# Hybrid attention encoder on one core: branch B's blocks and heads reordered and spaced, head normalisation on ScalarE, first two output blocks interleaved in K

## The chip, the core and the metric

One core of a Trainium2 chip runs the whole kernel. It has TensorE (PE: matmuls; PEld: its weight loads), VectorE (DVE), ScalarE (ACT), GpSimd (POOL) and SyncE (SP), which here issues every DMA. Each engine works through its own instructions strictly in the order in which the program gave them, and waits at an instruction until the semaphores that it needs have come. The metric is the device time of one execution in microseconds, the median over several runs.

## The reference, cut to what matters

256 tokens, width 2048, two layers, everything in float32. Each layer is

```python
h = rmsnorm(x, pre_norm_g[l])
proj = h @ w_in[l]                      # 2048 x 17920: q, k, v of three mixers, gates
ya = neighbourhood_attention(qa, ka, va, rpb[l])          # branch A, 8 heads
yb = gqa_attention(axial_rope(rmsnorm(qb)), axial_rope(rmsnorm(kb)), vb)   # branch B, 8 query heads, 2 key heads
yc = dilated_mixture(qc, kc, vc)                          # branch C, 4 output heads out of 12
merged = ga * ((ya * silu(za)) @ wa) + gb * ((yb * silu(zb)) @ wb) + gc * ((yc * silu(zc)) @ wc)
x = x + rmsnorm(merged @ w_out[l], post_norm_g[l])
```

where ga, gb, gc are sigmoids of the last 3 x 2048 columns of the projection. A head of branch A or B is a 256 x 256 score matrix, a softmax and a product with v.

## The kernel before, in words

**Blocks and chunks.** All large products go through one list, `stream` (L714 to L719). A block (`Blk`) makes 512 output columns for the 256 tokens, in two PSUM tiles `acc` of 128 tokens (T = 0 and 1); its K dimension is cut into chunks of 256 rows (`kc`). A chunk is one weight tile `raw` of 128x1024, which arrives by DMA and is split into a high part `wh` (ScalarE, L195) and a low part `wl` (VectorE, L200). Each chunk is twelve matmuls: two halves of K, two halves T, and three products high*high, low*high and high*low (`mm3`, L170 to L172). Numbered from 0, a layer has 352 chunks: ten blocks of branch C (chunks 0 to 79), eight of A (80 to 143), five of B (144 to 183), four merges of 34 chunks each (184 to 319: three gate blocks and the projections of branches A, C, B), and four output blocks (320 to 351).

**Order around the chunks.** The emission order is written out by hand. Before chunk i, `ahead(i)` (L203) emits the DMAs of `raw` up to chunk i+6, the `wh` of chunk i+3 and the `wl` of chunk i+2. After chunk i comes one `slot()` (L100): it takes up to two steps of the evacuations in `evq`, one step of each running job in `active`, and then starts one job: from `light` if one is due, otherwise from `heavy` if nothing is in `light` and the counter `cool` has come down to 0. The number that stands with a heavy job is the cool that follows it, the spacing of heads in chunks.

**A head** (`head_job`, L389; `job_c` for branch C) is a job whose steps lie one slot apart. Step 0: scores `sc` on TensorE, the row maximum `nm` on VectorE, two exponentials `sp` on ScalarE with their sums. Step 1: `norm` (L374), which makes `rsum` and multiplies the probabilities with it, on VectorE. Step 3: `turn` (L143), the transposition: VectorE transposes 32x32 squares into `tt`, a DMA writes `tt` to DRAM (`turn`), and at step 5 a DMA reads it back as `tx`. Step 7: `tx` is split into `pp` high and low. Step 9: the product `o` on TensorE, then `z` on VectorE; the fourth head of a unit also splits the gated result into `yTh` (ScalarE) and `yTl` (VectorE).

**`tr_job`** (L304) transposes a projected block in the same way (q, k, the gates, the merged tokens) and then, for branch B's queries, calls `then`, which puts the four heads of that block into `heavy`. `evac_qb` (L536) evacuates branch B's queries: four sums of squares on ScalarE (`junk`, L531), the mean `hss`, the rotary products `tok`, `s`, `tok` on VectorE (`rope`, L509) and the factor `bf`.

**Output blocks** (L628) read the merged tokens `mT`, one tile for each merge: chunk kc of any output block reads merge kc // 2. The last merge is transposed while the first output block runs.

Of the kernel before, what the change touches and what calls it, by code (L numbers as in the profile page):

```python
# [10 lines left out]
F32 = mybir.dt.float32  # L11
# [3 lines left out]
AF = mybir.ActivationFunctionType  # L15
ALU = mybir.AluOpType
# [4 lines left out]
P = 128  # L21
# [10 lines left out]
class Blk:  # L32


    def __init__(self, w, nk, stat, evac, pre=None):
        self.w, self.nk, self.stat, self.evac, self.pre = w, nk, stat, evac, pre
        self.nc = nk // 2
        self.lag = False
        self.far = False
        self.before = {}  # L40
        self.after = {}

# [5 lines left out]
def trunk(ctx, tc, x, xT, wpack, wbr_a, wbr_b, wbr_c, wout, pre_g, qk_g, bgate, post_g, abias,  # L48
          ident_d, rope_d, dist_d, x1, out):
    nc = tc.nc  # L50
# [4 lines left out]
    mm = ctx.enter_context(tc.tile_pool(name="mm", bufs=4, space=PSUM))  # L55
# [34 lines left out]
    evq, light, heavy, active = deque(), deque(), deque(), []  # L90
# [84 lines left out]
    stream = []  # L175
# [55 lines left out]
    def layer(l):  # L231
# [66 lines left out]
        def proj(nb, evac, pre=None):  # L298
            b = Blk([wpack[l, nb, kc] for kc in range(8)], 16, stat_h, evac, pre)
            blocks.append(b)  # L300
            return b


        def tr_job(dst, tok, n=4, then=None):  # L304


            tx = []
            yield from turn([tok[:, T] for T in range(2)], n, tx)
            for T in range(2):
                src = turned(tx[0], T, n)  # L310
                v = lambda t: squares(t[:, 0:n], T)
                if isinstance(dst, tuple):
                    split(src, v(dst[0]), v(dst[1]))
                else:
                    nc.scalar.copy(v(dst), src)
            if then:
                then()

        def evac_qk(store, key, which, two):
# [54 lines left out]
        def norm(p, sm, n, rsh):  # L374

            r = small.tile([P, n], F32, name="rsum")
            nc.vector.reciprocal(r, sm)
            nc.vector.tensor_tensor(out=r, in0=r, in1=rsh, op=ALU.mult)
            for i in range(n):
                nc.vector.tensor_scalar(p[:, i], p[:, i], r[:, i:i + 1], None, op0=ALU.mult)  # L380

        def gate(zb, hh, o, last):
            y = SZ[zb][:, hh]
# [40 lines left out]
        def job_a(u, hh, bias):  # L424
            q, k, v = QT["a", u], KT["a", u], V["a", u]
            d = slice(hh * P, (hh + 1) * P)
            return head_job(("a", u), hh, cols(q, ALL, hh), cols(k, ALL, hh),
                            lambda kk: cols(v, ALL, kk, d), bias=bias)

        def job_b(u, hh):  # L430
            d = slice(u * P, (u + 1) * P)
            return head_job(("b", u), hh, cols(QT["b", u], ALL, hh), cols(KT["b"], ALL, u),
                            lambda kk: cols(V["b"], ALL, kk, d), f=S["bf", u][:, hh])

        def job_c(hh, dist):

            q, k = [QT["c", g] for g in range(3)], [KT["c", g] for g in range(3)]
            v = [V["c", g] for g in range(3)]
            d = slice(hh * P, (hh + 1) * P)
            ps_ = []  # L440
            for T in range(2):
                c = slice(T * P, (T + 1) * P)
                sc = aux.tile([P, 1, 512], F32, name="sc")
                mm3(sc[:, 0, 0:256], cols(q[0], ALL, hh, c), cols(k[0], ALL, hh), True, True)
                for g in (1, 2):
                    nc.tensor.matmul(sc[:, 0, 128 + g * 128:256 + g * 128], lhsT=q[g][:, hh, c],  # L446
                                     rhs=k[g][:, hh, c], start=True, stop=True)
                sp = U("sp", [2, 1, 512])
                s, p = sp[:, 0], sp[:, 1]
                nc.vector.scalar_tensor_tensor(s[:, 0], dist[:, T], -(2.0 ** (-8.0 * (hh + 1) / 12)),  # L450
                                               sc[:, 0], op0=ALU.mult, op1=ALU.add)
                sm = softmax(s, p, 1, 512)
                ps_.append(p)
                yield
                norm(p, sm, 1, S["rsh"][T])
                if T == 0:
                    yield
            yield
            pp = U("pp", [2, 2, 256], FR)
            ph, pl = pp[:, 0], pp[:, 1]  # L460
            px = U("px", [2, 256])
            tx = []
            yield from turn([ps_[T][:, 0] for T in range(2)], 4, tx)
            for T in range(2):
                src = turned(tx[0], T, 4)
                split(src[:, 0:2], squares(ph, T), squares(pl, T))
                nc.scalar.copy(squares(px, T), src[:, 2:4])
            yield
            yield
            o = aux.tile([P, 256], F32, name="o")  # L470
            for kk in range(2):
                mm3(o, cols(v[0], ALL, kk, d), (ph[:, kk], pl[:, kk]), kk == 0, False)
            for T in range(2):
                c = slice(T * P, (T + 1) * P)
                for g in (1, 2):
                    nc.tensor.matmul(o[:, c], lhsT=v[g][:, T, d], rhs=px[:, g - 1, c],
                                     start=False, stop=T == 1 and g == 2)
            gate(("c", 0), hh, o, hh == 3)


        def a_unit(u):
            bias = {}

            def pre():
                for i in range(2):
                    b = U("abias", [2, 2, 256])
                    nc.sync.dma_start(out=b, in_=abias[l, u, i].rearrange("p (h t k) -> p h t k", h=2, t=2))
                    bias[i] = b

            def go():  # L490
                for hh in range(4):
                    heavy.append((2, job_a(u, hh, bias[hh // 2][:, hh % 2])))
            proj(18 + u, evac_z(("a", u)))
            proj(0 + u, evac_qk(QT, ("a", u), "rss", True))
            proj(2 + u, evac_qk(KT, ("a", u), "rs", True))
            proj(4 + u, evac_v(("a", u), True, go), pre=pre)
# [39 lines left out]
        def evac_qb(u):  # L536
            tok = {}

            def f(T, ps):
                if T == 0:  # L540
                    tok[0] = U("tok", [2, 512])
                    S["bf", u] = small.tile([P, 4, 2], F32, name="bf", bufs=2)
                    QT["b", u] = pair("qk", [4, 256])
                y = head_norm(ps, T, 4)
                yield from rope(tok[0][:, T], ps, T, 4, 0)
                nc.vector.tensor_scalar(S["bf", u][:, :, T], y, S["rss"][T], None, op0=ALU.mult)
                if T == 1:
                    later(tr_job(QT["b", u], tok[0],
                                 then=lambda: heavy.extend((2, job_b(u, hh)) for hh in range(4))), 1)
            return f  # L550

        def evac_kvb(T, ps):
# [17 lines left out]
        def go_c():  # L570
            dist = U("dist", [2, 512])
            nc.sync.dma_start(out=dist, in_=dist_d)
            for hh in range(4):
                heavy.append((4, job_c(hh, dist)))


        def merge(nb):
# [93 lines left out]
            proj(15 + g, evac_v(("c", g), g == 0, go_c if g == 2 else None))  # L671
        a_unit(0)
        a_unit(1)
        proj(20, evac_z(("b", 0)))
        b0 = proj(21, evac_z(("b", 1)))
        b0.at("after", (0, 1), b_tables)
        proj(8, evac_kvb)
        proj(6, evac_qb(0))
        proj(7, evac_qb(1))
        for nb in range(4):  # L680
            merge(nb)
        for nb in range(4):
            lastb = out_block(nb)
        lastb.lag = True

        if l == 0:
# [27 lines left out]
    for l in range(DEPTH):  # L714
        bl, S = layer(l)
        S0 = S0 or S
        for b in bl:
            for kc in range(b.nc):
                stream.append((b, kc))  # L719


    nc.sync.dma_start(out=gpre, in_=pre_g)
    for i in range(8):
        nb, k = divmod(i, 2)
# [23 lines left out]
    while i < len(stream):  # L748
        b = stream[i][0]
        n = b.nc  # L750
        if b.lag:
            a = [(i + k, 0) for k in range(n)]
            c = [(i + k, 1) for k in range(n)]
            order += a[:LAG]
            for k in range(n - LAG):
                order += [a[LAG + k], c[k]]
            order += c[n - LAG:]
        else:
            order += [(i + k, T) for k in range(n) for T in range(2)]
        i += n  # L760

    ps = {}
    for i, T in order:
        b, kc = stream[i]
        for f in b.before.get((kc, T), ()):
            f()
        if i > 0:
            ahead(i)
        if kc == 0:
            ps[T] = mm.tile([P, 512], F32, name="acc")  # L770
        run_half(i, T, ps[T])
        for f in b.after.get((kc, T), ()):
            f()
        if kc == b.nc - 1:
            evq.append(b.evac(T, ps[T]))
        if T == 1 or b.lag:
            slot()
    while evq or active or light:
# [99 lines left out]
```

## Time and profile before

| | before |
|---|---|
| median of 3 runs | 2043.8 us (2043.03 to 2046.01) |
| the profiled execution, whole | 2045.3 us |
| its span, first to last instruction | 2043.2 us |
| PE busy | 2014.1 us (99%) |
| VectorE busy | 1294.6 us (63%) |
| ScalarE busy | 959.0 us (47%) |
| mean granted TensorE clock | 0.994 |

The span is what the trace covers; 2.1 us lie around it. PE busy counts the time in which at least one matmul is under way, whatever clock it was granted, so that a slower stretch counts as busy too. The other engines' idle time matters only where TensorE waits for them.

### The profile page before, as it was taken

The page shows a single profiled execution, that of the slowest core. Times are in us where ns is not written, and L with a number is a line of the kernel's source. Part 1 is how long each engine was busy: PE and PEld are TensorE (multiplying, and loading weights), DVE is VectorE, ACT ScalarE, POOL GpSimd, SP SyncE. Part 2 cuts the span into 40 slices and gives each one's busy share as a digit, 9 for nine tenths or more (in the row PEclk, how much of TensorE's full clock was granted, in tenths as well). Part 3 has the DMA queues.
Part 4 walks back from the last instruction along what each step waited for, and adds up shares of the span by engine and source line. Part 5 has one row for each costly group of instructions (what it writes and reads, how often), then busy time and mean ns, then how long its engine had stood idle before and what let it go on. Part 6 is the DMA issues. An engine that isn't in the chain of part 4 may idle for free.

```text
span 2043.2 us, 24560 instructions
## 1 busy us (share of the span) xinstructions
PE 2014.1 (99%) x9098; PEld 1666.8 (82%) x9098; DVE 1294.6 (63%) x1645; ACT 959.0 (47%) x1402; POOL 24.0 (1%) x31
## 2 busy tenths in 40 slices
PE   9999999999999999999999999999999999999998
PEld 7888888888778888887888888888887788888876
DVE  6654587776786564645565555786767865646554
ACT  7544445445453444342564453555454544443422
POOL 0000000000000000000000000000000000000000
PEclk9999999999999999999999999999999999999999
DMA  8776375866666756667557664768665666656572
GB/s 326 258 263 258 137 287 203 290 215 257 217 215 225 263 199 218 226 212 272 185 167 275 240 249 144 277 226 303 211 259 191 240 217 245 217 195 225 201 283 72
DMA packets 171719, 468.05 MB, mean 229 GB/s; under 512 B 15440, under 2 KB 58576, under 8 KB 171600
## 3 DMA queue, kind: packets, MB, share of 16 engines
q1 hardware_dynamic: 171600, 466.50, 63.4%
q8 instruction: 71, 1.16, 0.2%
q14 instruction: 48, 0.39, 0.1%
HBM read 427.11 MB, written 39.32 MB: 228 GB/s over the span
## 4 chain that ended last, share of the span: by engine, by line
PE 89%; DVE 5%; ACT 2%; DMA 2%; issue 1%; SPq 0%; DVEq 0%; ACTq 0%; POOLq 0%
PE acc L171 29%; PE acc L172 29%; PE acc L170 29%; DMA tx<-turn 2%; DVE wl L200 1%; DVE tt L148 1%; ACT wh L195 1%; DVE nm L364 0%; ACT sp L369 0%; DVE pp L132 0%; PE sc L172 0%; PE sc L446 0%; DVE sp L380 0%; PE o L172 0%; PE o L171 0%
## 5 line engine op out<-in xcount | busy, mean ns | idle before, releaser
L200 DVE TENSOR_TENSOR wl<-raw,wh 128x1024 fp32r<-128x1024 f32 (+1 forms) x706 | 830.7, 1213 | 145.4 <-ACT wh L195 144.9
L171 PE MATMUL acc<-wl,hTh 128*128 128x512 f32 x2240 | 876.3, 391 | 7.4 <-DVE wl L200 7.4
L170 PE MATMUL acc<-wh,hTh 128*128 128x512 f32 x2240 | 877.4, 392 | 0.4 <-ACT wh L195 0.4
L172 PE MATMUL acc<-wh,hTl 128*128 128x512 f32 x2240 | 874.2, 390 | 0.0
L195 ACT CAST wh<-raw 128x1024 fp32r<-128x1024 f32 (+1 forms) x706 | 703.4, 1043 | 346.9 <-DMA raw<-in_wpack_dram 217.8
L171 PEld LDWEIGHTS acc<-wl,hTh 128*128 128x128 f32 x2240 | 422.2, 188 | 97.9 <-DVE wl L200 12.7
L172 PEld LDWEIGHTS acc<-wh,hTl 128*128 128x128 f32 x2240 | 422.1, 188 | 88.1
L170 PEld LDWEIGHTS acc<-wh,hTh 128*128 128x128 f32 x2240 | 422.3, 189 | 86.1 <-ACT wh L195 0.9
L170 PE MATMUL acc<-wh,yTh 128*128 128x512 f32 x320 | 124.5, 389 | 0.0
L171 PE MATMUL acc<-wl,yTh 128*128 128x512 f32 x320 | 124.5, 389 | 0.0
L172 PE MATMUL acc<-wh,yTl 128*128 128x512 f32 x320 | 124.5, 389 | 0.0
L594 ACT ACTIVATE g<-g 128x512 f32<-128x512 f32 x48 | 30.4, 634 | 192.8 <-DVE g L593 192.8
L593 DVE SCALAR_TENSOR_TENSOR g<-acc,rsx,bg 128x512 f32<-128x512 f32 x48 | 35.9, 747 | 128.7 <-PE acc L172 128.5
L170 PE MATMUL acc<-wh,mTh 128*128 128x512 f32 x256 | 101.6, 397 | 3.8 <-ACT mTh L130 3.8
L172 PE MATMUL acc<-wh,mTl 128*128 128x512 f32 x256 | 101.0, 395 | 0.0
L171 PE MATMUL acc<-wl,mTh 128*128 128x512 f32 x256 | 101.0, 394 | 0.0
L369 ACT ACTIVATE sp<-sp,nm 128x256 f32<-128x256 f32 (+1 forms) x48 | 27.6, 576 | 116.4 <-DVE nm L364 116.4
L605 DVE SCALAR_TENSOR_TENSOR g<-g,acc 128x512 f32<-128x512 f32 x48 | 32.8, 684 | 68.1 <-PE acc L172 68.1
L148 DVE STREAM_TRANSPOSE tt<-tok 128x512 f32<-128x512 f32 (+1 forms) x72 | 73.5, 1060 | 0.0
L171 PEld LDWEIGHTS acc<-wl,yTh 128*128 128x128 f32 x320 | 60.1, 188 | 12.4
L172 PEld LDWEIGHTS acc<-wh,yTl 128*128 128x128 f32 x320 | 60.1, 188 | 12.4
L170 PEld LDWEIGHTS acc<-wh,yTh 128*128 128x128 f32 x320 | 60.1, 188 | 12.3
(111 smaller groups left out, 1078.0 us busy)
## 6 DMA issues: line engine op xcount, KB each, us to landing
raw<-in_wpack_dram SPq DMA_DIRECT2D x558, 512.0 KB, 6.5
raw<-in_wo_dram SPq DMA_DIRECT2D x64, 512.0 KB, 9.2
turn<-tt SPq DMA_DIRECT2D x50, 512.0 KB, 3.0
tx<-turn SPq DMA_DIRECT2D x50, 512.0 KB, 5.5
raw<-in_wa_dram SPq DMA_DIRECT2D x32, 512.0 KB, 3.4
raw<-in_wb_dram SPq DMA_DIRECT2D x32, 512.0 KB, 4.6
turn<-tt SPq DMA_DIRECT2D x34, 256.0 KB, 2.2
tx<-turn SPq DMA_DIRECT2D x34, 256.0 KB, 4.3
```

Of the source, the lines that this page charges most:

```text
L148: nc.vector.transpose(out=tt[:, :, T].rearrange("p j (h a) -> p h j a", h=n), in_=srcs[T].rearrange("p (h b j) -> p h j b", h=n, j=4))
L170: nc.tensor.matmul(out_, lhsT=lh, rhs=rh, start=first, stop=False)
L171: nc.tensor.matmul(out_, lhsT=lh, rhs=rl, start=False, stop=False)
L172: nc.tensor.matmul(out_, lhsT=ll, rhs=rh, start=False, stop=last)
L195: nc.scalar.copy(HI[i][:, k], RAW[i][:, k])
L200: nc.vector.tensor_tensor(out=LO[i][:, k], in0=RAW[i][:, k], in1=f32(HI[i][:, k]), op=ALU.subtract)
L369: nc.scalar.activation(p[:, i], sc[:, i], AF.Exp, bias=nm[:, i:i + 1], scale=1.0 if f is None else f[:, i:i + 1], accum_out=sm[:, i:i + 1])
L593: nc.vector.scalar_tensor_tensor(g, ps, S["rs"][T], BG[i], op0=ALU.mult, op1=ALU.add)
L594: nc.scalar.activation(g, g, AF.Tanh, scale=0.5)
L605: nc.vector.scalar_tensor_tensor(G[i][:, T], G[i][:, T], 1.0, ps, op0=ALU.add, op1=ALU.mult)
```

## The change

1. `norm` multiplies the probabilities on ScalarE (an activation with function Copy and `rsum` as its scale) where it did on VectorE. `rsum` itself stays on VectorE.
2. The spacing of heads goes from 2 to 3 chunks in branches A and B, and from 4 to 5 in branch C.
3. `tr_job` waits two more slots between its split and `then`, so that branch B's first head comes two slots behind the split of its queries.
4. Branch B's blocks go from z0, z1, kv, q0, q1 to z0, kv, q0, z1, q1.
5. The first two output blocks are interleaved in K: six chunks of block 0, six of block 1, the last two of block 0, the last two of block 1.

```diff
             if then:
+                yield
+                yield
                 then()
...
             for i in range(n):
-                nc.vector.tensor_scalar(p[:, i], p[:, i], r[:, i:i + 1], None, op0=ALU.mult)
+                nc.scalar.activation(p[:, i], p[:, i], AF.Copy, scale=r[:, i:i + 1])
...
-                    heavy.append((2, job_a(u, hh, bias[hh // 2][:, hh % 2])))
+                    heavy.append((3, job_a(u, hh, bias[hh // 2][:, hh % 2])))
...
-                                 then=lambda: heavy.extend((2, job_b(u, hh)) for hh in range(4))), 1)
+                                 then=lambda: heavy.extend((3, job_b(u, hh)) for hh in range(4))), 1)
...
-                heavy.append((4, job_c(hh, dist)))
+                heavy.append((5, job_c(hh, dist)))
...
-        proj(20, evac_z(("b", 0)))
-        b0 = proj(21, evac_z(("b", 1)))
+        b0 = proj(20, evac_z(("b", 0)))
         b0.at("after", (0, 1), b_tables)
         proj(8, evac_kvb)
         proj(6, evac_qb(0))
+        proj(21, evac_z(("b", 1)))
         proj(7, evac_qb(1))
...
-        for nb in range(4):
-            lastb = out_block(nb)
+        outs = [out_block(nb) for nb in range(4)]
+
+        outs[0].mate, outs[1].mated = outs[1], True
+        lastb = outs[3]
...
         for b in bl:
-            for kc in range(b.nc):
-                stream.append((b, kc))
+            if b.mate:
+                m = b.mate
+                stream += [(b, kc) for kc in range(6)] + [(m, kc) for kc in range(6)]
+                stream += [(c, kc) for c in (b, m) for kc in range(6, 8)]
+            elif not b.mated:
+                stream += [(b, kc) for kc in range(b.nc)]
...
-            ps[T] = mm.tile([P, 512], F32, name="acc")
+            ps[b, T] = mm.tile([P, 512], F32, name="acc")
```

Branch B's second query block ends with chunk 183 in both. ScalarE's queue from the evacuation of its first half (the first four `junk`) is, before:

```order
L531 ACTIVATE junk,hss<-acc 128x128 x4
L130 ACTIVATE qkh<-tx 128x4x128 x2
L369 ACTIVATE sp,sm<-sc,nm,bf 128x256 x2
L195 CAST wh<-raw 128x1024
L531 ACTIVATE junk,hss<-acc 128x128 x4
L195 CAST wh<-raw 128x1024 x4
```

and in the changed kernel, from the exponentials of branch B's second head on:

```order
L373 ACTIVATE sp,sm<-sc,nm,bf 128x256 x2
L197 CAST wh<-raw 128x1024
L535 ACTIVATE junk,hss<-acc 128x128 x4
L384 ACTIVATE sp<-sp,rsum 128x256 x2
L197 CAST wh<-raw 128x1024
L535 ACTIVATE junk,hss<-acc 128x128 x4
```

The split of the first queries (`qkh`) and the first exponentials have left this place for an earlier one; the normalisation of the second head (L384) stands between the two groups of squares. VectorE's queue at the same place, in the changed kernel:

```order
L368 TENSOR_REDUCE nm<-sc 128x2
L370 TENSOR_TENSOR nm<-nm,bf 128x2
L202 TENSOR_TENSOR wl<-raw,wh 128x1024
L537 TENSOR_SCALAR hss<-hss,rsx 128x4
L517 TENSOR_TENSOR tok<-acc,ropeg 128x512
L525 TENSOR_TENSOR s<-acc,ropeg 128x8x32 x2
L527 TENSOR_TENSOR tok<-tok,s 128x512
L381 RECIPROCAL rsum<-sm 128x2
L382 TENSOR_TENSOR rsum<-rsum,rsx 128x2
L202 TENSOR_TENSOR wl<-raw,wh 128x1024
L550 TENSOR_SCALAR bf<-rs_y,rsx 128x4
L537 TENSOR_SCALAR hss<-hss,rsx 128x4
```

The second head's `rsum`, for which ScalarE's L384 waits, stands behind the rotary products of the first half. VectorE's queue where branch B's first unit ends (`yTl`), before:

```order
L384 TENSOR_TENSOR z<-o,z 128x256
L132 TENSOR_TENSOR yTl<-z,yTh 128x1024
L132 TENSOR_TENSOR pp<-tx,pp 128x2x128 x2
L148 STREAM_TRANSPOSE tt<-sp 128x2x4x32 x2
L377 RECIPROCAL rsum<-sm 128x2
L378 TENSOR_TENSOR rsum<-rsum,rsx 128x2
L380 TENSOR_SCALAR sp<-sp,rsum 128x256 x2
L200 TENSOR_TENSOR wl<-raw,wh 128x1024
```

and in the changed kernel:

```order
L388 TENSOR_TENSOR z<-o,z 128x256
L134 TENSOR_TENSOR yTl<-z,yTh 128x1024
L150 STREAM_TRANSPOSE tt<-sp 128x2x4x32 x2
L368 TENSOR_REDUCE nm<-sc 128x2
L370 TENSOR_TENSOR nm<-nm,bf 128x2
L202 TENSOR_TENSOR wl<-raw,wh 128x1024
L134 TENSOR_TENSOR pp<-tx,pp 128x2x128 x2
```

Between `z` and the next `wl` stand fewer instructions of other heads, and the two multiplications of L380 are gone. Counted in chunks, branch B's scores stand after chunks 183, 188, 190, 192, 194, 196, 198 and 200 before and after 179, 182, 188, 191, 194, 197, 200 and 203 in the changed kernel; the last `o` moves from chunk 209 to 212, and its `yT` is first read in chunk 216 in both.

## Rows read from the trace of the kernel before

**Rows 1.** The page: busy time of each engine, and the chain by engine.

```profile
PE 2014.1 (99%) x9098; PEld 1666.8 (82%) x9098; DVE 1294.6 (63%) x1645; ACT 959.0 (47%) x1402; POOL 24.0 (1%) x31
PE 89%; DVE 5%; ACT 2%; DMA 2%; issue 1%; SPq 0%; DVEq 0%; ACTq 0%; POOLq 0%
```

**Rows 2.** Stretches: length, busy time of each engine, then PEclk, DMA share, GB/s.

```profile
300.00:318.00 18.00, 17.01 (x81) 13.68 (x80) 13.27 (x15) 11.32 (x16) 0.00 (x0) 1.00 0.56 211
534.00:540.00 6.00, 3.27 (x15) 2.21 (x15) 4.21 (x10) 2.15 (x9) 1.01 (x1) 1.00 0.90 353
571.00:614.00 43.00, 39.26 (x185) 32.15 (x184) 35.75 (x70) 25.15 (x49) 0.00 (x0) 0.96 0.65 220
942.00:952.00 10.00, 8.04 (x27) 5.81 (x27) 3.67 (x5) 4.29 (x8) 0.00 (x0) 0.83 1.03 403
1315.00:1333.00 18.00, 17.40 (x82) 14.00 (x81) 13.23 (x15) 11.33 (x16) 0.00 (x0) 1.00 0.58 219
1548.00:1560.00 12.00, 9.28 (x35) 7.01 (x34) 6.42 (x15) 7.00 (x25) 1.58 (x2) 0.86 0.55 215
1600.00:1632.00 32.00, 28.96 (x129) 23.39 (x128) 24.57 (x48) 18.81 (x34) 0.00 (x0) 0.89 0.63 217
1959.00:1969.00 10.00, 8.18 (x28) 5.91 (x28) 3.61 (x5) 4.30 (x8) 0.00 (x0) 0.83 1.04 402
```

**Rows 3.** TensorE's waits: for whom, us in total, times, longest.

```profile
PE acc L171 <- DVE wl L200: 7.4, 11, 2.0
PE acc L170 <- ACT mTh L130: 3.8, 2, 2.0
PE sc L172 <- DVE qkl L132: 3.7, 2, 1.8
PE sc L170 <- ACT qkh L130: 1.8, 2, 0.9
PE o L171 <- DVE pp L132: 1.7, 2, 0.9
```

**Rows 4.** Timeline of TensorE: one chunk's first matmul and the next chunk's.

```profile
545.07 0.39 PE L170 MATMUL acc<-wh,hTh 128*128 128x512 f32 x1
545.30 0.39 PE L171 MATMUL acc<-wl,hTh 128*128 128x512 f32 x1
...
547.79 0.39 PE L170 MATMUL acc<-wh,hTh 128*128 128x512 f32 x1
```

**Rows 5.** Chain of waits at branch A's first queries: start, us, what.

```profile
291.34 1.98 DVE tt L148 x2
...
293.77 6.13 DMA tx<-turn
```

**Rows 6.** Timeline of ScalarE: squares and first exponentials, then the last merge.

```profile
533.64 0.28 ACT L531 ACTIVATE junk<-acc 128x128 f32<-128x128 f32 x1 [2.17 <-PE acc L172]
...
535.11 1.14 ACT L130 ACTIVATE qkh<-tx 128x512 fp32r<-128x512 f32 x2
...
541.22 1.04 ACT L195 CAST wh<-raw 128x1024 fp32r<-128x1024 f32 x1
...
944.17 1.15 ACT L130 ACTIVATE mTh<-tx 128x512 fp32r<-128x512 f32 x2 [1.74 <-DMA tx<-turn]
```

**Rows 7.** Timeline of VectorE around branch B's first heads.

```profile
513.46 0.23 DVE L533 TENSOR_SCALAR hss<-hss,rsx 128x4 f32<-128x4 f32 x1 [5.26 <-ACT junk L531]
...
515.59 0.75 DVE L132 TENSOR_TENSOR kb<-tx,kb 128x256 fp32r<-128x256 f32 x2
...
539.14 0.69 DVE L364 TENSOR_REDUCE nm<-sc 128x2 f32<-128x512 f32 x1 [0.48 <-PE sc L172]
...
544.50 0.16 DVE L377 RECIPROCAL rsum<-sm 128x2 f32<-128x2 f32 x1
...
544.89 0.62 DVE L380 TENSOR_SCALAR sp<-sp,rsum 128x256 f32<-128x256 f32 x2
...
549.21 1.13 DVE L148 STREAM_TRANSPOSE tt<-sp 128x256 f32<-128x256 f32 x2
```

**Rows 8.** Groups by shape: busy us, mean ns of one, idle before.

```profile
L200 DVE TENSOR_TENSOR wl<-raw,wh 128x1024 fp32r<-128x1024 f32 x702 | 827.9, 1216 | 145.2 <-ACT wh L195 144.7 <-issue 0.3
L380 DVE TENSOR_SCALAR sp<-sp,rsum 128x256 f32<-128x256 f32 x64 | 19.7, 351 | 1.1
L326 ACT ACTIVATE tok<-acc,rsx 128x512 f32<-128x512 f32 x40 | 27.4, 685 | 67.6 <-PE acc L172 67.6
L566 ACT ACTIVATE tok<-tok,kf 128x128 f32<-128x128 f32 x8 | 2.8, 395 | 7.3 <-DVE kf L563 7.3
```

More of the change, by code (lines that the diff above doesn't have):

```diff
@@ L39, in __init__ @@
         self.far = False
+        self.mate = None
+        self.mated = False
         self.before = {}
@@ L758, in trunk @@
         else:
-            order += [(i + k, T) for k in range(n) for T in range(2)]
+            n = 1
+            order += [(i, T) for T in range(2)]
         i += n
@@ L769, in trunk @@
         if kc == 0:
-            ps[T] = mm.tile([P, 512], F32, name="acc")
-        run_half(i, T, ps[T])
+            ps[b, T] = mm.tile([P, 512], F32, name="acc")
+        run_half(i, T, ps[b, T])
         for f in b.after.get((kc, T), ()):
@@ L774, in trunk @@
         if kc == b.nc - 1:
-            evq.append(b.evac(T, ps[T]))
+            evq.append(b.evac(T, ps.pop((b, T))))
         if T == 1 or b.lag:
```

## Prediction

> **What bounds the kernel now.** I read the page first. TensorE is busy for 99% of the span, and the chain that ended last runs through it for 89%; VectorE has 5% of it and ScalarE 2% [rows 1]. So no engine can be made the bound by a few per cent, and nothing is to be had beside TensorE's own losses. There are two kinds of those: waits, and stretches in which its clock was granted at less than full speed, which the page counts as busy. I therefore cut the span into the stretches where the list of TensorE's waits says it waited inside the layers, and read two columns: length less PE busy is idle time, and length times (1 - PEclk) is time lost to the lower of the two clock levels, 1.2 GHz in place of 2.4 [rows 2].
>
> A third loss hides in the pitch. A full chunk takes 547.79 - 545.07 = 2.72 us, so a matmul starts every 0.227 us while each row shows 0.39 [rows 4]; 0.16 us of the next one lie under it, and each wait costs that much more than its idle time.
>
> Whom TensorE waits for says what each place is: `wl` from VectorE in eleven waits, the last merge's `mTh` in two, branch B's first scores (`qkh`, `qkl`) in four, a head's `pp` in two [rows 3]. Three of the eleven belong to the start and to the border between the layers, which the change leaves alone. The clock was lower only after waits: after each of the two of about 2.0 us for `mTh`, in both layers at the end of branch B's heads, and after branch B's first scores in the second layer, not in the first (PEclk 0.86 in 1548 to 1560, 1.00 in 534 to 540) [rows 2, 3].
>
> The losses by place, both layers, idle + 0.16 a wait + clock [rows 2, 4]:
> - before branch A's first heads (300 to 318, 1315 to 1333): 0.99 + 0.60 + 4 x 0.16 = 2.2 us;
> - branch B's first scores (534 to 540, 1548 to 1560): 2.73 + 2.72 + 4 x 0.16 + 12 x 0.14 = 7.8 us;
> - branch B's later heads (571 to 614, 1600 to 1632): 3.74 + 3.04 + 7 x 0.16 + 43 x 0.04 + 32 x 0.11 = 13.1 us;
> - first output block (942 to 952, 1959 to 1969): 1.96 + 1.82 + 2 x 0.16 + 2 x 10 x 0.17 = 7.5 us.
>
> Together 30.6 us. This is what the change can win, and nearly all that there is.
>
> **The change part by part.**
>
> *Output blocks.* The last merge is first needed in the seventh chunk of block 0. Interleaving puts six chunks of block 1 ahead of it: 6 x 2.72 = 16.3 us against a wait of 2.0. What could keep the stall alive is ScalarE's order: the split `mTh` stays where it was in its queue, waits 1.74 us there for `tx` [rows 6], and the `wh` of three chunks later stand behind it. But `wl` of two chunks is ready at that point. Had TensorE not waited, it would need the next `wl` 2 x 2.72 + 0.23 = 5.7 us after the point at which it now stops; splitting the merge (1.2 us on ScalarE, another 0.7 on VectorE until its second half, by the same sizes) and one `wl` (1.2) come to about 2.0 + 1.2 + 0.7 + 1.2 = 5.1 us. That fits, barely. I take all 7.5 us back.
>
> *Branch A's first queries.* `tx` of these queries takes 6.13 us and is issued late, because a head of branch C stands ahead of it on SP's queue and its transposition only ends at 291.34 + 1.98 [rows 5]. With branch C's spacing at 5, that head's transposition comes three chunks later, behind this `tx`; the second wait of the pair, where the last head of branch C, its `yT` and a projection's transposition stood together ahead of one `wl`, is taken apart as well. 2.2 us back.
>
> *Branch B's later heads.* Per head VectorE has the maximum, `rsum`, the two transposed halves, `pp`, `z` and, before, two multiplications of 0.35 us [rows 7, 8]: some 3.9 us with the multiplications (estimated from these rows, `pp` and `z` at the multiplication's width taken at 0.35 to 0.4). With two `wl` of 1.2 that is 6.3 us, in 2 x 2.72 us and 1.4 of scores and product (twelve matmuls of half the columns), 6.8 us. That leaves nothing for gates and rotary products, so `wl` falls behind for eight heads on end. With spacing 3 and without the multiplications it is 3.4 + 3 x 1.2 = 7.0 in 9.6 us. At the worst place left (`yTl` of the first unit) I add up the queue again and find `wl` late by 0.2 us a layer. 13.1 - 0.4 us back.
>
> *Branch B's first scores.* They now stand two slots behind the split of their queries, and the queries a block earlier, so the wait for `qkh` and `qkl` goes: 7.8 us back.
>
> *What is added.* The evacuation of the second query block now meets branch B's second head in flight, and there ScalarE's new multiplication waits for `rsum`, which stands on VectorE behind the rotary products. Time 0 is the start of chunk 183, right behind the scores; the reduction starts at 0.2.
> - ScalarE is through with the exponentials 541.22 - 539.14 = 2.1 us after the reduction's start [rows 6, 7]: 2.3. One `wh`, some 0.95: 3.2. Four squares, 535.11 - 533.64 = 1.47 [rows 6]: 4.7.
> - VectorE from `hss` to the end of the rotary products, 515.59 - 513.46 = 2.13: 6.8. `rsum`, 0.39: 7.2 [rows 7]. `wl` of chunk 186, 1.2 [rows 8]: 8.4. TensorE needs it at 3 x 2.72 + 0.23 = 8.4. No loss yet.
> - ScalarE: the two multiplications. No row shows one; the nearest are Copy activations with a scale from memory, 0.395 us at 128 columns and 0.685 at 512 [rows 8], the bounds for one. I take 0.49 by the straight line between them, 0.9 for the overlapping pair: 8.1. `wh` 9.0, squares of the other half 10.5.
> - VectorE: `hss` and the first product, a third of the 2.13: 11.2. `wl` of chunk 187: 12.4, needed at 11.1. Late by 1.3.
> - Then the rest of the rotary products (1.4), `bf`, the first head's transposed halves (1.1 [rows 7]) and `wl` of chunk 188: 16.2, needed at 12.4 + 2.72 = 15.1. Late by 1.1.
>
> That is 2.4 us a layer, 4.8 in all, and behind it the clock may go down as it did behind half of the comparable places: I count one layer of two, 1.7 us. With the bounds for a multiplication and none or both of the clock losses, this term lies between 3 and 11 us.
>
> Elsewhere the multiplications cost TensorE nothing: 80 x 0.5 = 40 us more on ScalarE, which is busy 47%, are covered by its idle time, and the two slots between `norm` and the transposition, 5.4 us, cover the way from `rsum` over ScalarE to VectorE. If that cover is gone, VectorE's `tt` is late, and with it SP, which stands at `turn` with the `raw` loads behind it.
>
> **A rule against this change.** VectorE's multiplication takes 0.351 us, ScalarE's by the rows 0.49 [rows 8]. The Trainium skill, "ScalarE: Activation LUTs", section "Rules for kernel authors", gives multiplications to VectorE and not to ScalarE. On the length of one instruction the trace sides with it: 64 x 0.14 = 9 us more engine time (and more for branch C). By the rule alone the change would lose by that; by the rows it moves work from the engine for which TensorE waits to the one that waits itself.
>
> **The sum.** 2043.2 - 30.6 + 4.8 + 1.7 + 0.4 = 2019.5 us of span, 2.1 around it: 2021.6 for an execution like the profiled one (2045.3). That one lay 1.5 above the median of the runs, so 2020.1.
>
> **The rivals.**
> - *All waits go.* VectorE's queue has more air at chunk 186 than my sum gives it (it was even there). Then 2043.8 - 30.6 = 2013.
> - *The new wait spreads.* Three other places came out with less than half a microsecond to spare (the evacuation of keys and values, now beside branch A's last head; the second unit's queries; `yTl`). If each is late by 1.2 us in each layer, with the clock down behind half of them: 6 x (1.2 + 0.85) = 12 us more, 2032.
> - *ScalarE's order keeps the output stall.* If the next `wl` misses its 5.7 us, the 7.5 us stay: 2027.6.
> - *ScalarE's longer multiplication is paid in full*, the rule above as a mechanism: every `tt` waits for it, 9 us for A and B and 3 for C: 2032. Against it: ScalarE's share of the chain is 2%.
> - *Slower.* `norm` holds ScalarE at every one of the 40 heads as it does at chunk 186, because `rsum` comes last in VectorE's step everywhere. At 1.2 us a head that is 48 us: 2043.8 - 30.6 + 48 = 2061. It decides from 0.76 us a head on. Against it: in the plain step (split, `rsum`, `wl`) I find 0.9 us or more to spare.
> - *No change*: gains and new waits cancel.
>
> **How the numbers follow.** My forecast 0.60 (2016 to 2025 with the bounds of its term), all waits gone 0.11, the wait spreads 0.13, output stall 0.05, multiplication paid 0.04, no change 0.03, slower 0.04. A range of 2013 to 2030 holds the forecast, the first rival, the output stall and a part of the spread: about 8 in 10. This kernel's runs tell 0.2% (4 us) from no change: faster 0.93, same 0.03, slower 0.04.
>
> **What would show it.** Right: no wait for `mTh` or for branch B's `qkh`; two waits of about 1 us for `wl` near chunks 187 and 188 of each layer, with ScalarE idle before L384 for about 2.5 us; none before branch A's first heads; ScalarE's busy time up by about 40 us, VectorE's down by the 19.7 of L380 [rows 8] and branch C's share. Wrong: a wait for `wl` at many heads (slower or spread), PEclk under 1.00 at more than two places, or a wait at chunk 328, two behind the split of the merge.

## The result, and the profile after

The changed kernel takes 2019.65 us (median of 4 runs, 2018.62 to 2020.04) against 2043.41 us for the kernel before on the same chip (4 runs, 2040.7 to 2046.01): a ratio of 0.9884, interval 0.9868 to 0.9899, so faster by 1.2%. Forecast: 2020.1 us by the sum, range 2013 to 2030. The profiled execution took 2019.99 us, 2.1 us more than its span of 2017.9; the sum had 2021.6 and 2019.5. Line numbers have moved: L200 is now L202, L195 is L197, L380 (VectorE) is L384 (ScalarE).

The page after, busy time and chain, as in [rows 1]:

```profile
PE 2002.0 (99%) x9098; PEld 1660.7 (82%) x9098; DVE 1271.1 (63%) x1565; ACT 995.9 (49%) x1482; POOL 21.5 (1%) x31
PE 92%; DVE 3%; ACT 3%; DMA 1%; issue 0%; SPq 0%; DVEq 0%; POOLq 0%; ACTq 0%
```

ScalarE has 36.9 us more, VectorE 23.5 less. Of the 25.3 us that the span lost, 12.1 come out of TensorE's "busy" time (2014.1 to 2002.0) and the rest out of its waits, so the waits alone don't tell the gain.

The places of [rows 2] in the new execution, where they come somewhat earlier and branch B's heads spread further (the columns are the same):

```profile
300.00:318.00 18.00, 18.00 (x86) 15.07 (x85) 12.62 (x13) 9.93 (x14) 0.00 (x0) 1.00 0.71 252
525.00:560.00 35.00, 33.18 (x152) 26.86 (x151) 25.39 (x46) 20.30 (x50) 2.01 (x2) 1.00 0.59 204
560.00:614.00 54.00, 53.73 (x265) 45.21 (x265) 40.89 (x70) 34.69 (x65) 0.00 (x0) 1.00 0.66 232
928.00:950.00 22.00, 22.00 (x98) 18.21 (x97) 12.11 (x12) 10.20 (x11) 0.00 (x0) 1.00 1.01 387
1315.00:1333.00 18.00, 18.00 (x90) 15.23 (x89) 11.93 (x14) 9.99 (x15) 0.00 (x0) 1.00 0.90 350
1530.00:1563.00 33.00, 31.16 (x144) 25.19 (x143) 23.92 (x42) 18.94 (x46) 2.01 (x2) 1.00 0.56 199
1563.00:1618.00 55.00, 54.65 (x269) 46.07 (x268) 41.62 (x71) 34.39 (x64) 0.00 (x0) 1.00 0.66 230
1932.00:1956.00 24.00, 24.00 (x108) 19.87 (x107) 11.10 (x11) 10.41 (x11) 0.00 (x0) 1.00 1.00 381
```

Idle time is length less PE busy: none at branch A's first heads and at the output, 1.82 and 1.84 us in the stretches of branch B's first heads (525 to 560, 1530 to 1563), 0.27 and 0.35 in those of its later heads, where the first unit's `yTl` is made. PEclk is 1.00 in all of them. The list of TensorE's waits, to be held against [rows 3]:

```profile
PE acc L173 <- DVE wl L202: 5.1, 9, 1.2
PE acc L89 <- DVE warm L86: 1.5, 1, 1.5
PE acc L172 <- ACT wh L197: 0.6, 1, 0.6
PE tp L142 <- DVE x L627: 0.3, 2, 0.2
```

`mTh`, `qkh`, `qkl` and `pp` are gone from it.

**The new wait.** VectorE at chunks 186 to 188 of the first layer (start, us, instruction, in brackets the idle time before it and what ended it):

```profile
540.34 0.16 DVE L382 TENSOR_TENSOR rsum<-rsum,rsx 128x2 f32<-128x2 f32 x1
540.42 1.22 DVE L202 TENSOR_TENSOR wl<-raw,wh 128x1024 fp32r<-128x1024 f32 x1
...
543.88 0.23 DVE L537 TENSOR_SCALAR hss<-hss,rsx 128x4 f32<-128x4 f32 x1 [2.10 <-ACT junk L535]
...
544.62 1.22 DVE L202 TENSOR_TENSOR wl<-raw,wh 128x1024 fp32r<-128x1024 f32 x1
...
548.37 1.18 DVE L202 TENSOR_TENSOR wl<-raw,wh 128x1024 fp32r<-128x1024 f32 x1
```

and ScalarE there:

```profile
540.54 0.91 ACT L384 ACTIVATE sp<-sp,rsum 128x256 f32<-128x256 f32 x2 [2.55 <-DVE rsum L382]
...
543.65 0.20 ACT L535 ACTIVATION_READ_ACCUMULATOR junk<-acc 128x1 f32 x1
```

Chunk 183 begins at 533.20, and counted from there the forecast's clockwork can be read off: `rsum` ends at 7.3 (forecast 7.2), `wl` of chunk 186 at 8.4 (8.4), the squares of the second half at 10.6 (10.5), `wl` of chunk 187 at 12.6 (12.4), `wl` of chunk 188 at 16.3 (16.2). TensorE waits 1.16 us for the second of these `wl` (list above, longest 1.2) and 0.66 for the third.

**The chain at `yTl`** (start, us, what), which ends in the other wait left:

```profile
586.80 0.76 DVE pp L134 x2
...
587.67 0.17 DVE rsum L382
...
587.93 0.91 ACT sp L384 x2
588.84 0.96 ACT wh L197
...
591.74 0.63 ACT g L598
592.37 0.96 ACT yTh L132
...
593.36 1.22 DVE yTl L134
594.58 1.05 DVE tt L150 x2
...
596.32 1.23 DVE wl L202
```

The multiplication L384 is a link of it: `rsum` stands behind the `pp` of the head before, the multiplication behind `rsum`, and `wh`, the gate's `g` and `yTh` behind the multiplication.

### The profile page after: what moved, and what is told of

Its sections match the earlier page's. It is cut to its first block, busy times and chain, and to the rows that moved or that the text cites. A ratio compares the mean times of both kernels' runs of the same rounds, so it can differ in the third digit from the quotient of the medians.

```text
span 2017.9 us, 24528 instructions
## 1 busy us (share of the span) xinstructions
PE 2002.0 (99%) x9098; PEld 1660.7 (82%) x9098; DVE 1271.1 (63%) x1565; ACT 995.9 (49%) x1482; POOL 21.5 (1%) x31
## 3 DMA queue, kind: packets, MB, share of 16 engines
q8 instruction: 71, 1.16, 0.2%
## 4 chain that ended last, share of the span: by engine, by line
PE 92%; DVE 3%; ACT 3%; DMA 1%; issue 0%; SPq 0%; DVEq 0%; POOLq 0%; ACTq 0%
PE acc L173 30%; PE acc L174 30%; PE acc L172 30%; ACT wh L197 1%; DVE wl L202 1%; DVE tt L150 1%; ACT sp L373 1%; PE o L174 0%; PE o L173 0%; PE o L172 0%; ACT sp L384 0%; DMA raw<-in_wpack_dram 0%; PE sc L174 0%; PE sc L450 0%; PE o L480 0%
## 5 line engine op out<-in xcount | busy, mean ns | idle before, releaser
L202 DVE TENSOR_TENSOR wl<-raw,wh 128x1024 fp32r<-128x1024 f32 (+1 forms) x706 | 833.7, 1214 | 169.9 <-ACT wh L197 169.7
L197 ACT CAST wh<-raw 128x1024 fp32r<-128x1024 f32 (+1 forms) x706 | 706.2, 1042 | 268.4 <-DMA raw<-in_wpack_dram 155.3
```

The source lines that it names most:

```text
L197: nc.scalar.copy(HI[i][:, k], RAW[i][:, k])
L202: nc.vector.tensor_tensor(out=LO[i][:, k], in0=RAW[i][:, k], in1=f32(HI[i][:, k]), op=ALU.subtract)
```

## Experiments

All start from the changed kernel ("after") or from a variant of it named there; interleaving and the spacings of branches A and C stay unless said. Ratios are to the kernel before, run on the same chip. The kernel before had medians of 2043.41, 2044.41, 2045.52 and 2047.07 us beside these runs, so medians taken beside different ones of them are compared by their ratios; each span, and each trace, is one execution.

| run | edit | median us | ratio, interval | span us |
|---|---|---|---|---|
| after | - | 2019.65 | 0.9884 (0.9868 to 0.9899) | 2017.9 |
| x0_after | after again | 2020.44 | 0.9881 (0.9864 to 0.9897) | 2019.1 |
| x1_norm_dve | multiplication on VectorE | 2015.95 | 0.9853 (0.9839 to 0.9866) | 2014.1 |
| x2_b2 | B's heads 2 apart | 2023.11 | 0.9886 (0.9872 to 0.9899) | 2019.1 |
| x7_dve_b2 | both of these | 2023.83 | 0.9889 (0.9874 to 0.9904) | 2020.9 |
| x3_no_mix | no interleaving | 2028.9 | 0.9915 (0.9902 to 0.9929) | 2024.5 |
| x9_c4 | C's heads 4 apart | 2025.97 | 0.9898 (0.9884 to 0.9913) | 2025.3 |
| x5_no_late | no yields | 2030.69 | 0.9922 (0.9907 to 0.9936) | 2028.9 |
| x4_rsum_first | `rsum` ahead of the evacuations | 2013.57 | 0.9840 (0.9827 to 0.9854) | 2011.6 |
| x15_rsum_first_twice | x4, multiplication doubled | 2018.03 | 0.9867 (0.9851 to 0.9883) | 2014.6 |
| x6_order_b2 | blocks as before, B 2 apart | 2013.48 | 0.9838 (0.9822 to 0.9855) | 2011.0 |
| x8_order_b2_dve | x6, multiplication on VectorE | 2026.71 | 0.9911 (0.9894 to 0.9927) | 2024.9 |
| x13_order_b2_no_late | x6, no yields | 2023.27 | 0.9893 (0.9874 to 0.9911) | 2021.0 |

**Two parts undone that have a place of their own.** x3:

```
-        outs[0].mate, outs[1].mated = outs[1], True
```

> After with output blocks 0 and 1 one after the other again. Theory A (the interleaving alone took the wait for the last merge's mTh, with the clock loss behind it): the wait of 2.0 us and the clock's 1.7 return in both layers, 7.5 us: 2027.2 us (2026 to 2028.5). Theory B (earlier heads also bring the last merge forward, or the clock falls only by chance): 2020 to 2025.

The wait for `mTh` came back in both layers, the clock loss behind it in the second alone:

```profile
934.00:944.00 10.00, 8.26 (x36) 6.20 (x35) 4.31 (x6) 5.55 (x8) 0.00 (x0) 1.00 1.04 403
1940.00:1952.00 12.00, 9.55 (x36) 7.46 (x35) 5.32 (x7) 5.61 (x11) 0.00 (x0) 0.86 1.03 403
```

Idle 1.74 and 2.45, 0.32 for the pitch, 12 x 0.14 of clock: 6.2 us here, where 7.5 stood before. Most of the rest of the span's 6.6 us is one wait of about half a microsecond at the second unit's queries. Theory A, with the median 0.4 us above its range: the profiled execution is the shortest of five (2026.5 us against 2028.36 to 2029.19), at a mean granted clock of 0.998 against 0.997 in the others.

x9:

```
-                heavy.append((5, job_c(hh, dist)))
+                heavy.append((4, job_c(hh, dist)))
```

> After with branch C's heads four slots apart again. Theory A (branch C's spacing alone moved the head's transposition behind the queries' tx): waits for wl return near 303 and 316 us and near 1318 and 1331 us, 0.4 to 0.9 us each, 2.2 us in all: span 2020.1 us, 2021 to 2023 in time. Theory B (branch A's spacing or the multiplication did it): no wait there, span 2018.

Both waits came back, in both layers; the stretch of the first layer and that of the second:

```profile
300.00:324.00 24.00, 21.70 (x94) 17.33 (x94) 14.85 (x16) 11.31 (x16) 0.00 (x0) 0.93 0.56 205
...
1305.00:1330.00 25.00, 24.04 (x118) 19.65 (x117) 16.23 (x18) 12.50 (x18) 0.00 (x0) 1.00 0.71 264
```

That is 2.30 + 0.32 + 24 x 0.07 = 4.3 us and 0.96 + 0.32 = 1.3 us, more than the 2.2 of before, because the first wait was longer in one layer and the clock fell behind it. This execution is the longest of four (the others took 2023.57 to 2026.98 us). Theory A, missed in size. SyncE's row of that `tx` in after:

```profile
290.50 0.38 SPq L159 DMA_DIRECT2D tx<-turn  x1
```

It was issued at 290.50, where [rows 5] has it at 293.77 and x9 at 295.79, in both right behind a head's `turn`.

**The yields.** x5 takes them out of after, x13 out of x6:

```
             if then:
-                yield
-                yield
                 then()
```

> After without the two yields between the split of the queries and the release of the heads. Theory A (the yields took the wait for qkh and qkl): at chunk 178 of each layer TensorE waits for qkl again, 1.3 us (two products of 0.65 us on VectorE behind one of 0.7), with the clock down behind one of them perhaps, and the pile at chunks 186 to 188 gets about 1 us worse a layer because the first head is three slots further: 2023 to 2028 us. Theory B (the earlier query block alone took it, the split being long done): 2019 to 2021.

> x6 without the two yields: blocks in the order of before, two slots apart, multiplication on ScalarE. Theory A (the yields take the first scores' wait and ScalarE's multiplication the later heads'): the first scores' 7.8 us come back, the second unit's with up to 7 more (x5), the later heads stay without waits: 2020 to 2028 us. Theory B (the yields did both): the later heads' 13 us come back as well, 2032 us or more.

In x13 the first scores wait as before, almost to the hundredth of [rows 2] (9.28 busy and PEclk 0.86 in 12 us), now in both layers, and branch B's later heads don't wait:

```profile
532.00:544.00 12.00, 9.28 (x34) 6.98 (x34) 6.38 (x14) 6.02 (x23) 1.50 (x2) 0.86 0.54 216
1538.00:1550.00 12.00, 9.28 (x36) 7.24 (x35) 7.35 (x16) 6.59 (x25) 2.01 (x2) 0.86 0.47 182
573.00:612.00 39.00, 39.00 (x198) 33.25 (x197) 33.14 (x60) 27.67 (x55) 0.00 (x0) 1.00 0.72 239
```

2.72 + 2.72 + 4 x 0.16 + 2 x 12 x 0.14 = 9.4 of the 10.0 us by which its span exceeds x6's. The second unit's scores, for which I had allowed up to 7 us, did not wait. In x5 the first unit's scores cost little, the second unit's much:

```profile
510.00:517.00 7.00, 6.70 (x31) 5.10 (x30) 3.58 (x6) 2.46 (x6) 0.00 (x0) 1.00 1.04 406
564.00:576.00 12.00, 9.32 (x38) 7.25 (x37) 8.91 (x16) 8.28 (x15) 0.00 (x0) 0.86 0.75 260
```

I had expected 1.3 us at the first and had not counted the second, so the time is above my range: with after's order the first unit's heads have all been started when the second unit's queries are split, and its scores stand right behind the split. So the yields are needed in either order of the blocks.

**The multiplication, the spacing and the order of the blocks.** The edits are

```
-                nc.scalar.activation(p[:, i], p[:, i], AF.Copy, scale=r[:, i:i + 1])
+                nc.vector.tensor_scalar(p[:, i], p[:, i], r[:, i:i + 1], None, op0=ALU.mult)
```

for x1,

```
-    then=lambda: heavy.extend((3, job_b(u, hh)) for hh in range(4))), 1)
+    then=lambda: heavy.extend((2, job_b(u, hh)) for hh in range(4))), 1)
```

for x2, and

```
+        proj(20, evac_z(("b", 0)))
+        b0 = proj(21, evac_z(("b", 1)))
-        b0 = proj(20, evac_z(("b", 0)))
...
-        proj(21, evac_z(("b", 1)))
```

for x6, which also has x2's spacing, since with the old order and three slots the second unit's last head would be issued behind the merge that reads it. x7 has the first two edits, x8 all three.

> After with the multiplication by rsum back on VectorE, all else kept. Theory A (with heads three slots apart VectorE has room for the two multiplications, and the wait at chunks 186 to 188 is ScalarE's wait for rsum): ScalarE's idle 2.5 us before the squares of the second half goes, wl(186) is late by about 0.7 and wl(188) by 0.5 instead of 1.3 and 0.8, so about 1 us a layer is won there and up to 0.5 a layer lost where yTl is made: 2016.5 to 2019.5 us. Theory B (it is the move to ScalarE that cured branch B's later heads): waits for wl return in 571 to 614 and 1600 to 1632, up to 13 us: 2028 to 2033.

> After with branch B's heads two slots apart again, the multiplication staying on ScalarE. Theory A (VectorE's sum per head decides: about 3.2 us and two wl in 6.8 us without the multiplications): later heads without waits; only chunks 186 to 188 get worse, because a third head's reduction stands behind the rotary products there, wl(187) late by some 3.4 us, the place costing 4 us a layer in place of 2.5: 2022 to 2027 us. Theory B (spacing alone cured the later heads): the 13 us of the later heads come back as well: 2032 or more.

> After with both the multiplication back on VectorE and branch B's heads two slots apart; order of blocks, yields and interleaving kept. Each of the two alone left no wait at the later heads (x1, x2). Theory A (VectorE's sum per head against the time between heads; either is enough, without both it overflows): waits for wl and pp return between chunk 198 and 210 of each layer, 5 to 13 us more than x2: 2028 to 2036 us. Theory B (the later heads were cured by something else, the order of the blocks say): as x2, 2021 to 2025.

> After with branch B's blocks in the order of before (with it the heads only fit two slots apart, so they stand so; to be compared with x2). Theory A (the yields alone take the wait for the first scores, and VectorE has room at two slots once the multiplication is on ScalarE): no wait for qkh, no head in flight at chunks 186 to 188, so x2's 3.0 us a layer there go, and waits of about 0.5 us come at two or three later heads a layer, which are more crowded together: 2018 to 2022 us. Theory B (the order is needed for the first scores or the later heads): 2026 or more.

> x6 (blocks in the order of before, two slots apart, yields kept) with the multiplication back on VectorE. From chunk 194 to 204 its VectorE queue is that of before but for yTl, a head later. Theory A (with the order of before the two multiplications on VectorE are what makes wl late at the later heads, as the prediction's sum of 6.3 us in 6.8 has it): waits for wl and pp between chunk 198 and 208 come back, most of the 13.1 us: 2021 to 2027 us. Theory B (the yields cured the later heads by moving them away from a gate's evacuation): 2013 to 2016 us.

The stretch of the later heads (columns as before) in x2, first layer:

```profile
575.00:614.00 39.00, 39.00 (x193) 33.05 (x192) 29.35 (x50) 24.74 (x46) 0.00 (x0) 1.00 0.74 261
```

The same in x7:

```profile
575.00:614.00 39.00, 38.62 (x190) 32.49 (x189) 30.40 (x57) 22.14 (x39) 0.00 (x0) 1.00 0.70 249
```

In x6, both layers, first heads included:

```profile
525.00:614.00 89.00, 89.00 (x433) 75.08 (x432) 70.68 (x122) 54.45 (x114) 2.01 (x2) 1.00 0.71 242
...
1525.00:1618.00 93.00, 93.00 (x453) 78.57 (x452) 74.33 (x128) 58.37 (x120) 2.01 (x2) 1.00 0.73 253
```

In x8, both layers:

```profile
575.00:612.00 37.00, 33.66 (x160) 27.45 (x160) 31.63 (x64) 20.39 (x40) 0.00 (x0) 0.96 0.61 210
1582.00:1618.00 36.00, 32.65 (x158) 26.65 (x157) 30.63 (x63) 19.48 (x40) 0.00 (x0) 0.97 0.62 211
```

With the old order the multiplication decides: on ScalarE no idle time (x6), on VectorE 3.34 and 3.35 us of it with the clock down in both layers (x8), and a span that is 13.9 us longer. The idle time does not come at all eight heads: in x8's first layer it is four waits, of 0.52, 0.49, 0.30 and 2.03 us, and the longest, 2.03 in both layers, is for the `wl` behind `yTl`, as it was in the kernel before. Rows of VectorE and TensorE there:

```profile
601.14 0.42 DVE L388 TENSOR_TENSOR z<-o,z 128x256 f32<-128x256 f32 x1
603.30 1.23 DVE L134 TENSOR_TENSOR yTl<-z,yTh 128x1024 fp32r<-128x1024 f32 x1 [1.75 <-ACT yTh L132]
...
608.37 0.50 PE L173 MATMUL acc<-wl,hTh 128*128 128x512 f32 x1 [2.03 <-DVE wl L202]
```

The same `z` in x6:

```profile
597.41 0.42 DVE L388 TENSOR_TENSOR z<-o,z 128x256 f32<-128x256 f32 x1 [0.17 <-PE o L174]
```

So VectorE falls behind over the heads and TensorE pays mostly at one place: `z` starts 3.4 us after the first matmul of its product in x8 (597.74), 0.9 in x6 (596.50).

With the new order the multiplication does not decide that: even with the heads two slots apart and the multiplication on VectorE only 0.38 us of the first layer's idle time is left, and 0.40 of the second's (x7). So theory A held for x8 and failed for x7. With the new order the two units no longer run together: in x7 five chunks lie between the third head of the first unit and the fourth and five more between that and the second unit's first, where x8 has all eight two chunks apart. That this distance is what spares x7 is read from the order of the program and was not tried by itself.

With the new order and the heads three slots apart the multiplication on VectorE is the better one: x1 has a span 3.8 us shorter than after and is faster than theory A's 2016.5. Its ScalarE starts the second half's squares at 538.38, after's at 542.29; TensorE's only wait for branch B is one of 0.6 us a layer, and the one at `yTl` is gone. Two slots apart the place of the multiplication makes no difference clear of noise (x2 and x7: ratios 0.9886 and 0.9889).

x2, whose later heads don't wait as its theory A had it, and x6 show what the new order costs: a head in flight at chunks 186 to 188. x2 there:

```profile
540.00:555.00 15.00, 12.17 (x50) 9.58 (x49) 12.43 (x24) 9.54 (x23) 1.01 (x1) 0.89 0.51 165
1545.00:1560.00 15.00, 12.18 (x59) 9.83 (x58) 12.44 (x24) 9.54 (x23) 1.01 (x1) 1.00 0.52 165
```

x6's rows above hold the same chunks and all heads of branch B: no idle time, full clock. I had expected it to lose half a microsecond at two or three crowded heads; it lost nothing.

**Is it `rsum`'s place?** x4 leaves everything as in after and only lets the reciprocal and product of `rsum` (L381, L382) be issued at the start of the slot, ahead of the evacuations' steps, at every head (cut to branches A and B, branch C's is alike):

```
         flow["slot"] += 1
+        while early:
+            early.pop()()
         while evq and n and not flow["hold"]:
...
+        def rsum(sm, n, rsh):
+            r = small.tile([P, n], F32, name="rsum")
+
+            def f():
+                nc.vector.reciprocal(r, sm)
+                nc.vector.tensor_tensor(out=r, in0=r, in1=rsh, op=ALU.mult)
+            early.append(f)
+            return r
...
-            sm = softmax(s, p, 2, 256, f=f)
+            sm = rsum(softmax(s, p, 2, 256, f=f), 2, S["rsh2"])
```

> After with reciprocal and product of rsum issued at the start of a slot, before the evacuations, all else kept. Theory A (the wait at chunks 186 to 188 comes of rsum standing behind the rotary products): ScalarE's idle 2.5 us there shrinks to under 1, wl(187) is in time and wl(188) late by about 0.3; 2 us a layer are won: 2015 to 2016.5 us. Theory B (VectorE's work at chunks 186 to 188 is too much in any order): the waits move but stay, 2019 to 2020.5.

x4's VectorE at chunks 186 and 187:

```profile
535.33 0.16 DVE L387 TENSOR_TENSOR rsum<-rsum,rsx 128x2 f32<-128x2 f32 x1
...
541.66 1.22 DVE L206 TENSOR_TENSOR wl<-raw,wh 128x1024 fp32r<-128x1024 f32 x1
```

Its ScalarE there:

```profile
537.39 0.90 ACT L395 ACTIVATE sp<-sp,rsum 128x256 f32<-128x256 f32 x2
```

Counted from the head's reduction (532.90 here, 533.40 in after) `rsum` is done 4.5 us earlier, the multiplication waits for nothing, `wl` of chunk 187 starts at 541.66 in place of 544.62. The same instructions in another order, and the waits go at both places, `yTl` included; the span is 6.3 us shorter than after's, more than the 4 I expected, and 5.2 of it are the waits at these two places. Theory A.

**Is the multiplication paid?** x15 adds to x4

```
+                nc.scalar.activation(p[:, i], p[:, i], AF.Copy, scale=1.0)
```

> x4 (rsum first) with a second activation on ScalarE behind each multiplication, a copy with scale 1.0 in place, so the suspected cost of 40 us of ScalarE's time stands twice. Theory A (it is covered by ScalarE's idle time, and two slots stand behind it): same as x4 within 2 us at most, a little lost at chunks 186 to 188: 2013.5 to 2016. Theory B (the longer multiplication is paid, every transposition waits for it): 9 us or more, over 2022.

ScalarE's busy time rose by 35.4 us (995.2 to 1030.6), the span by 3.0, all in waits for `wl` at two places a layer, the two of after (chunk 188 and `yTl`):

```profile
540.00:550.00 10.00, 9.43 (x44) 7.52 (x43) 9.35 (x17) 5.23 (x11) 1.01 (x1) 1.00 0.30 69
590.00:600.00 10.00, 8.91 (x46) 7.26 (x45) 6.58 (x12) 6.76 (x15) 0.00 (x0) 1.00 0.56 203
```

Neither theory as I had put it: idle time covers nine tenths of it, and the rest is paid where TensorE has no slack. The median rose by 4.5 us, above theory A's 2016.

**After again, beside these.**

> The changed kernel again, beside these on one chip. As before, waits of 2.5 us at chunks 186 to 188 and 0.6 where yTl is made, in each layer: 2018 to 2021 us, 6 us over x4.

As expected, but for one more wait: 15.00 - 14.62 = 0.38 us at the second unit's queries in the first layer:

```profile
560.00:575.00 15.00, 14.62 (x73) 12.11 (x72) 11.91 (x21) 9.83 (x17) 0.00 (x0) 1.00 0.73 251
```

This is one of the three places that the forecast named as having less than half a microsecond to spare; it waits in some executions and not in others.

## Why the prediction was right

| term (both layers) | forecast us | measured us |
|---|---|---|
| losses of before removed at the four places | 30.6 | 30.6 (no wait of before is left there) |
| new wait, chunks 186 to 188 | 4.8 | 1.82 + 1.84 + 4 x 0.16 = 4.3 |
| `yTl` | 0.4 | 0.27 + 0.35 + 2 x 0.16 = 0.9 |
| clock behind the new wait | 1.7 | 0 (PEclk 1.00 in both layers) |
| span | 2019.5 | 2043.2 - 30.6 + 4.3 + 0.9 = 2017.8; profile 2017.9 |

- **The output's 7.5 us: right.** In after the blocks that held the stall show no idle time and full clock; x3 puts the stall back. ScalarE's order did not keep it: no wait followed two chunks behind the split.
- **Branch A's first queries, 2.2 us: right,** and for the reason given: branch C's spacing alone brings the waits back (x9).
- **Branch B's first scores, 7.8 us: right in size, half right in reason.** The two slots do it, in either order of the blocks (x5, x13); the query block's earlier place, which I named beside them, is not needed (x6).
- **Branch B's later heads, 13.1 us: right in size; the reason holds for the old order of blocks alone.** That VectorE falls behind in the old order, and that the multiplications decide it, holds: x6 and x8 differ by them alone, and by 13.9 us. But `wl` was not late "for eight heads on end": most of the idle time is one wait behind `yTl`. And I gave the win to the spacing and the multiplication together, while with the new order neither was needed but for 0.4 us a layer (x1, x2, x7). So two cures were applied to one loss: the multiplication (x6) and, nearly enough by itself, the order of the blocks (x7), to which I had credited nothing here. Whether the spacing alone would do is not shown.
- **The new wait: right,** in place, mechanism and size (4.3 for 4.8), and x4 shows the mechanism by `rsum`'s place alone. The step that was off is the clock term, "I count one layer of two": none of the two fell. The span's difference, 1.6 us, is about this term, because 4.3 for 4.8 here and 0.9 for 0.4 at `yTl` cancel. That the median came still closer (2019.65 for 2020.1) is luck: the sum took 1.5 us off for the place of the profiled execution among the runs, and here that is 0.3.
- **`yTl`: mis-sized,** 0.9 for 0.4. I added up VectorE's queue and left out that the multiplication on ScalarE is a link of that chain.
- **"Elsewhere the multiplications cost TensorE nothing": nearly.** The estimate of 0.49 us for one was good; the groups by shape show 502 ns. ScalarE stands idle before them for 23.2 us in all, 0.58 us for each of the 40 heads, and TensorE waits in branches A, B and C only at the two places above, 5.2 us in all. So the rival that ends slower, which needed 0.76 us of TensorE's time at every head, was far off:

```profile
L384 ACT ACTIVATE sp<-sp,rsum 128x256 f32<-128x256 f32 x64 | 29.0, 502 | 18.2 <-DVE rsum L382 18.2
...
L384 ACT ACTIVATE sp<-sp,rsum 128x512 f32<-128x512 f32 x16 | 11.6, 722 | 5.0 <-DVE rsum L382 5.0
```

- **The rule against the change** had a point that I took too lightly. The Trainium skill, "ScalarE: Activation LUTs", "Rules for kernel authors", gives multiplications to VectorE. The runs agree for the kernel as changed (x1 is 3.8 us of span better), disagree for the old order of blocks (x8 is 13.9 worse than x6) and don't tell for the new order at two slots (x2, x7). The 9 us by which the instructions are longer do not decide it: in x15 35.4 us more on ScalarE cost 3.0 of span.

Two versions are the fastest: x4 (2013.57 us, 2013.02 to 2013.8) and x6 (2013.48 us, 2013.27 to 2013.53), 0.984 of the kernel before. They reach the forecast's "all waits go" at 2013 by different ways: x6 leaves the blocks where they were, x4 keeps their new order and mends what it brought.

What stays open: why the second unit's queries wait in some executions (x0, x3, x9) and not in others. VectorE's queue there is the same; no run was made for it.

## What to carry to other kernels

When an instruction is moved to an engine with idle time, look at what it waits for there and what is queued behind it: a second multiplication cost a tenth of its length on ScalarE, and the first cost most where its operand stood behind a long step on VectorE, and letting two instructions of 0.16 us go first at every head won 6.3 us. The same move was worth 13.9 us, nothing clear of noise or minus 3.8 us by the order of the blocks and the spacing of the heads around it, so of several edits aimed at one stall, undo each by itself before keeping them all. A sum over the queues of both engines, from row to row at the one place where two steps meet, foretold ends to a quarter of a microsecond; at `yTl`, where the other engine's links were left out, it found less than half of what was measured.

## What the runs showed of the hardware

The length of one wait does not settle whether TensorE's clock falls to the lower of its two levels behind it. The pair of waits at chunks 186 to 188 (1.2 and 0.7 us) was never followed by it, in any of the ten layers of after, x0, x3, x5 and x9. In x2 the wait at the same place (one of 2.83 and 2.82 us) left PEclk at 0.89 in the first layer's stretch and at 1.00 in the second's (x7 shows the same two values there); in x3 a wait of about 1.7 us left it at 1.00 and one of 2.4 at 0.86. A price for it in a forecast is a chance, and belongs in the range more than in the sum.
